# A two-layer decoder on one core: attention outputs turned, stored and split 18 to 22 chunks later, turned queries read two chunks later, one mask product on GpSimd

## The chip, the core and the metric

The kernel runs on one core of a Trainium2 chip. TensorE (PE) multiplies, with weight loads (PEld) beside the matmuls; VectorE (DVE), ScalarE (ACT) and GpSimd (POOL) do the elementwise work; SyncE (SP) issues the transfers. The metric is the device time of one execution in microseconds (us); less is better.

## The reference

A batch of one sequence of 256 tokens passes through two layers, all in f32. What matters here is the mixer of a layer:

```
proj = rms_norm(x) @ w_in          # 2048 -> 5632: q, k, v and four HGRN2 parts
q, k = rope(q), rope(k)            # 16 query heads, 4 key heads of 64
attn = rms_norm(sliding_window_attention(q, k, v, sinks), attn_gain)
f = lb + (1 - lb) * sigmoid(hf);  k_in = (1 - lb) * sigmoid(-hf)
o = hgrn2_chunkwise(silu(hq), k_in, hi, log f)     # gated linear recurrence, 8 heads of 128
hgrn = rms_norm(o, hgrn_gain) * silu(hg)
m = concat([attn, hgrn]) @ w_out   # then norm, residual, gated feed-forward, input embeddings
```

Attention has a window of 128: with 256 tokens in two blocks, block 0 sees its own keys, and block 1 sees its own keys under a lower triangle and those of block 0 under an upper one.

## The kernel before

Tokens stand in two tiles of 128 rows (t = 0 and 1). Every weight matrix is cut into strips of 512 columns, and a strip into chunks of 256 rows (512 KB). `load_w` (L264) loads a chunk into one of 4 raw buffers `wr`, ACT casts it to a rounded half `wh` (L174), and DVE subtracts to get the rest, `wl` (L175); there are 8 buffers of each half. `strip` (L274) runs 12 matmuls of 512 columns per chunk: for two k-tiles and two token tiles, activation-high by weight-high (L286), activation-low by weight-high (L287) and activation-high by weight-low (L289). So PE can go on with a chunk only when its cast and its subtraction are done; below, the subtraction of chunk n is called sub n, and chunks are counted from the start of a layer's input projection. Chunks 0 to 7 are keys and values, 8 to 23 queries (two halves of 8 heads), 24 to 31 the gate f of the first group of recurrence heads, 32 to 39 its q, 40 to 47 its i, 48 to 55 its g, and 56 to 87 the same for the second group.

All the rest of a layer is woven into the strips. `tick` (L94) is called once per chunk; `later(n, fn)` traces `fn` n ticks later, and generators started with `start` do one piece per tick. The order in which each engine runs its instructions is then set by a list scheduler: what is traced earlier has the higher priority, and an instruction goes where its inputs and its buffers allow it in the scheduler's own reckoning. A step that is traced later is therefore not held until then; it only gives way to what is traced ahead of it. Each engine executes its list in order, and SP's queue too.

A turn of data (`shuffled`, L208) is a transpose of 32x32 blocks on DVE (L215 or L218), a store to DRAM (L225) and four fetches (L231) that bring the blocks to their places. `attend` (L538), one generator per half and token tile, turns the queries, copies them into `qT` (L542), computes scores (L570), exponentials (L593), turns these, multiplies them by the masks in `masked` (L605; for t = 1 a product with `m_low` and one with `m_up`, both on DVE at L612), multiplies by the values (L621) and scales into `ao` (L624). After the second half it takes the norm, scales `ao` into two buffers (L551), turns them, and `split_shuffled` (L246) splits them into the high and low operands `ck` of the output projection: 4 products on ACT (L254) and 4 on DVE (L255) for each of the two buffers and each t. These operands are first read at the output projection, after chunk 87.

The recurrence (`Rec`, L637) turns f by transposes on PE (L657) into `f` and `k` by two sigmoids on ACT (L659, L660) and products on DVE (L663, L665), turns q (L680) into `qd`, and goes through doubling levels: L769, L772 and L774; L732 and L741 for levels 2 and 8, after `up` and `prepare` (L701 to L721); L797 for 32 and 64; L804; then outputs (L823, L824). `ao` shares its two buffers with the recurrence's `q` and `qd`, and `qT` with its `f` and `k`. The buffers `nat` for all passing data are 12, the PSUM buffers `ms` for all small matmuls 4.

Of the kernel before, what the change touches and what calls it, by code (L numbers as in the profile page):

```python
# [12 lines left out]
ALU = mybir.AluOpType  # L13
AX = mybir.AxisListType

P = 128
# [30 lines left out]
def decoder(ctx: ExitStack, tc: tile.TileContext, x, p, positions, w_in, attn_sinks,  # L47
# [16 lines left out]
    V, S, G, T = nc.vector, nc.scalar, nc.gpsimd, nc.tensor  # L64

    def tiny(n):
        return sm.tile([P, n], F32, tag="tiny", name="tiny", bufs=16)
# [4 lines left out]
    def later(n, fn):  # L72

        queue.append((clock[0] + n, fn))
# [3 lines left out]
    @contextmanager  # L78
    def behind(*names):

        with ExitStack() as st:
            for n in names:
                st.enter_context(tc.issue_after(marks[n].ins))
            yield
# [18 lines left out]
    def nat(shape=(P, W), dt=F32):  # L103
        return np_.tile(list(shape), dt, tag="nat", name="nat")

    def bank(shape=(P, W)):
        return pms.tile(list(shape), F32, tag="ms", name="ms")
# [38 lines left out]
    def gain_cols(base, l, n):  # L146
        return gT[:, base + l * n: base + (l + 1) * n]
# [24 lines left out]
    def split(src, hi, lo):  # L172

        a = S.copy(hi, src)  # L174
        v = V.tensor_tensor(lo, src, hi.bitcast(F32), op=ALU.subtract)  # L175
        return a, v
# [27 lines left out]
    def turn_order(a):  # L204

        return a.rearrange("p (q k i) -> p k q i", q=4, k=4)

    def shuffled(src, n=4, slow=True, ready=False):  # L208

        if ready:
            b = src
            V.transpose(b, b)  # L215
        else:
            b = nat((P, n * P))
            V.transpose(b.rearrange("p (q k j) -> p k q j", q=4, k=n),  # L218
                        src.rearrange("p (k q j) -> p k q j", k=n, q=4))
        m = dp.tile([4, 32, 4, n * 32], F32, tag="turn", name="turn")  # L220
        got = []

        def store():
            with behind("pe") if slow else nullcontext():
                nc.sync.dma_start(m.rearrange("a i q f -> (a i) (q f)"), b)  # L225

        def fetch():
            d = nat((P, n * P))
            with behind("pe") if slow else nullcontext():
                for q in range(4):  # L230
                    nc.sync.dma_start(d[q * 32:(q + 1) * 32].rearrange("i (a f) -> i a f", a=4),  # L231
                                      m[:, :, q].rearrange("a i f -> i a f"))
            got.append(d.rearrange("p (a k j) -> p k a j", a=4, k=n))
        if slow:
            later(1, store)
            later(2, fetch)
        else:
            store()
            fetch()
        return got  # L240

    def quarters(a):

        return a.rearrange("p k (a j) -> p k a j", a=4)

    def split_shuffled(d, gcols, hl, t):  # L246
        d, = d
        h, lo = (quarters(a[:, :, t * P:(t + 1) * P]) for a in hl)
        if gcols is None:
            split(d, h, lo)  # L250
            return
        for b in range(4):
            g = gcols[:, b:b + 1]
            marks["x"] = S.activation(h[:, b], d[:, b], AF.Copy, scale=g)  # L254
            V.scalar_tensor_tensor(lo[:, b], d[:, b], g, h[:, b].bitcast(F32),  # L255
                                   op0=ALU.mult, op1=ALU.subtract)
# [93 lines left out]
    m_low = cp.tile([P, P], F32, name="m_low")  # L350
    m_up = cp.tile([P, P], F32, name="m_up")
# [129 lines left out]
    for l in range(DEPTH):  # L481
# [55 lines left out]

        def attend(half, t, o):  # L538
            d = shuffled(o, ready=True)
            for _ in range(6):  # L540
                yield
            S.copy(quarters(qT[half][:, :, t * P:(t + 1) * P]), d[0])  # L542
            yield
            yield from head_pair(half, t)
            if half == 1:
                yield
                r = sum_rstd(ssa[t], 1024, f"ra{t}")
                d = []
                for h in range(2):
                    b = nat()  # L550
                    V.tensor_scalar(turn_order(b), ao[t][:, h].rearrange("p (k q i) -> p k q i", k=4, q=4),  # L551
                                    r[:, 0:1], None, op0=ALU.mult)
                    d.append(shuffled(b, ready=True))
                for _ in range(5):
                    yield
                for h in range(2):
                    split_shuffled(d[h], gain_cols(96, l, 8)[:, 4 * h:4 * h + 4], attn[h], t)

        def head_pair(half, t):

            q = qT[half]
            blocks = [t] if t == 0 else [t, t - 1]
            sc = {}
            for u in blocks:
                for g in range(2):
                    sc[u, g] = bank((P, 4, P))
                for j in range(4):
                    for g in range(2):
                        rows = slice(g * 64, (g + 1) * 64)
                        T.matmul(sc[u, g][:, j], q[rows, j, t * P:(t + 1) * P],  # L570
                                 kT[rows, half, u * P:(u + 1) * P], start=True, stop=True)
            ex, dens = [], []
            for g in range(2):
                kv = 2 * half + g
                hs = slice(kv * 4, kv * 4 + 4)
                st = nat()
                s_ = turn_order(st)

                def four(a):
                    return a.rearrange("p j (q i) -> p j q i", q=4)  # L580
                if t == 0:
                    V.tensor_tensor(s_, four(sc[t, g]),
                                    four(m_neg.unsqueeze(1)).to_broadcast([P, 4, 4, 32]), op=ALU.add)
                else:
                    S.copy(s_, four(sc[t, g]))
                    V.copy_predicated(s_, four(m_prev.bitcast(I32).unsqueeze(1))
                                      .to_broadcast([P, 4, 4, 32]), four(sc[t - 1, g]))
                nm = tiny(4)
                V.tensor_reduce(nm, s_, axis=AX.XY, op=ALU.max, negate=True)
                V.tensor_tensor(nm, nm, nsink[:, l, hs], op=ALU.min)  # L590
                den = tiny(4)
                for j in range(4):
                    S.activation(s_[:, j], s_[:, j], AF.Exp, bias=nm[:, j:j + 1],  # L593
                                 accum_out=den[:, j:j + 1])
                es = tiny(4)
                V.tensor_tensor(es, sink[:, l, hs], nm, op=ALU.add)
                S.activation(es, es, AF.Exp)
                V.tensor_tensor(den, den, es, op=ALU.add)
                V.reciprocal(den, den)
                ex.append(shuffled(st, ready=True))  # L600
                dens.append(den)
                if g == 0:
                    yield

            def masked(g):  # L605
                ec = nat((P, 4, P))
                if t == 0:
                    S.copy(quarters(ec), ex[g][0])
                    return [(t, ec)]
                ep = nat((P, 4, P))  # L610
                for e, m in ((ec, m_low), (ep, m_up)):
                    V.tensor_tensor(quarters(e), ex[g][0], quarters(m.unsqueeze(1))  # L612
                                    .to_broadcast([P, 4, 4, 32]), op=ALU.mult)
                return [(t - 1, ep), (t, ec)]

            def values(g, parts):
                kv = 2 * half + g
                po = bank((P, 4, 64))
                for j in range(4):
                    for i, (u, e) in enumerate(parts):  # L620
                        T.matmul(po[:, j], e[:, j], vv[:, u, kv * 64:(kv + 1) * 64],  # L621
                                 start=i == 0, stop=i == len(parts) - 1)
                dst = ao[t][:, half, g * 256:(g + 1) * 256]
                V.tensor_tensor(dst.rearrange("p (j d) -> p j d", d=64), po,  # L624
                                dens[g].unsqueeze(2).to_broadcast([P, 4, 64]), op=ALU.mult)
                square_sum(dst, ssa[t][:, kv:kv + 1], (P, 256))

            for _ in range(4):
                yield
            p0 = masked(0)  # L630
            yield
            values(0, p0)
            p1 = masked(1)
            yield
            values(1, p1)
# [375 lines left out]
```

## Time and profile before

| | |
|---|---|
| median of 3 runs | 2454.04 us (2452.37 to 2454.14) |
| the profiled execution | 2453.65 us, span 2451.9 us |
| PE busy | 2429.4 us (99%) |
| DVE, ACT, POOL busy | 1486.0, 1184.7, 101.2 us |
| DMA | 497.59 MB, mean 203 GB/s |
| granted TensorE clock, mean | 0.999 of full speed |

The two layers are at 0 to about 1250 us and from there to the end. The attention and the first group of the recurrence lie at 83 to 235 us in the first layer and at 1295 to 1445 us in the second. A matmul of 512 columns shows as 0.39 us of PE, but one starts every 0.23 us, since they are pipelined; busy time of PE therefore hides short waits, and its idle time is what is left of a wait after the pipeline has run dry.

### The profile page before, as it was taken

To read this page: it belongs to the slowest core of one execution; us is meant where nothing else is said; L and a number is where in the kernel's file an instruction comes from. 1 tells how busy PE (TensorE), PEld (TensorE's weight loads), DVE (VectorE), ACT (ScalarE), POOL (GpSimd) and SP (SyncE) were. 2 spreads that over 40 slices of the span, in tenths; PEclk is the share of its full clock that TensorE was granted. 3 is DMA by queue.
4 is the path that set the end of the run, shared out by engine and by line. 5 is a ranking of instruction groups with operands and counts; after the bars stand their busy time and mean duration, and the time that the engine had idled before them with its cause. 6 is when DMAs were issued, how large, how long until landed. Compare 5 with 4: busy or idle time off the path is not lost.

```text
span 2451.9 us, 30895 instructions
## 1 busy us (share of the span) xinstructions
PE 2429.4 (99%) x11245; PEld 2006.4 (82%) x11245; DVE 1486.0 (61%) x1991; ACT 1184.7 (48%) x1684; POOL 101.2 (4%) x213
## 2 busy tenths in 40 slices
PE   9999999999999999999999999999999999999999
PEld 7888887888888888887888888878888888888877
DVE  7678756554555555557666877565545555555674
ACT  6465445444444444446555554464444444344463
POOL 3100001000000000001010000010000000000010
PEclk9999999999999999999999999999999999999999
DMA  8657465766767766774776674657767677667754
GB/s 264 218 181 219 141 198 154 233 220 202 214 205 211 211 211 195 226 221 154 249 222 195 194 226 144 200 182 217 225 191 229 192 212 212 209 207 214 221 170 129
DMA packets 299064, 497.59 MB, mean 203 GB/s; under 512 B 23424, under 2 KB 68896, under 8 KB 298912
## 3 DMA queue, kind: packets, MB, share of 16 engines
q1 hardware_dynamic: 298608, 495.54, 66.0%
q8 instruction: 88, 1.44, 0.2%
q14 instruction: 64, 0.52, 0.1%
q10 hardware_dynamic: 240, 0.07, 0.0%
q0 software_dynamic: 64, 0.02, 0.0%
HBM read 470.38 MB, written 25.17 MB: 202 GB/s over the span
## 4 chain that ended last, share of the span: by engine, by line
PE 93%; DVE 3%; DMA 1%; ACT 1%; issue 1%; POOL 0%; SPq 0%; DVEq 0%; ACTq 0%; POOLq 0%
PE acc L286 30%; PE acc L287 30%; PE acc L289 29%; DMA wr<-in_w_in_dram 1%; PE ms L621 1%; PE ms L732 1%; DVE wl L175 1%; PE ms L189 0%; PE ms L570 0%; ACT junk L170 0%; PE ms L797 0%; ACT wh L174 0%; DVE ck L255 0%; PE ms L287 0%; PE ms L286 0%
## 5 line engine op out<-in xcount | busy, mean ns | idle before, releaser
L175 DVE TENSOR_TENSOR wl<-wr,wh 128x1024 fp32r<-128x1024 f32 x840 | 1024.4, 1223 | 839.2 <-ACT wh L174 831.1
L174 ACT CAST wh<-wr 128x1024 fp32r<-128x1024 f32 x840 | 882.1, 1053 | 1073.6 <-PE acc L287 919.7
L286 PE MATMUL acc<-wh,ck 128*128 128x512 f32 x3328 | 1302.2, 392 | 8.3 <-ACT ck L200 5.8
L289 PE MATMUL acc<-wl,ck 128*128 128x512 f32 x3328 | 1296.7, 390 | 5.0 <-DVE wl L175 5.0
L287 PE MATMUL acc<-wh,ck 128*128 128x512 f32 x3328 | 1300.3, 391 | 0.9 <-DVE ck L201 0.8
L286 PEld LDWEIGHTS acc<-wh,ck 128*128 128x128 f32 x3328 | 625.5, 188 | 143.9 <-ACT ck L200 10.8
L289 PEld LDWEIGHTS acc<-wl,ck 128*128 128x128 f32 x3328 | 625.8, 188 | 136.0 <-DVE wl L175 7.5
L287 PEld LDWEIGHTS acc<-wh,ck 128*128 128x128 f32 x3328 | 625.8, 188 | 134.4 <-DVE ck L201 4.4
L200 ACT ACTIVATE ck<-ms,gT 128x128 fp32r<-128x128 f32 x176 | 55.7, 369 | 25.4 <-DVE ck L201 15.2
L201 DVE SCALAR_TENSOR_TENSOR ck<-ms,gT,ck 128x128 fp32r<-128x128 f32 x176 | 53.8, 347 | 16.8 <-ACT ck L200 16.3
L160 POOL TENSOR_TENSOR tiny<-ssf 128x1 f32<-128x1 f32 x4 | 2.1, 536 | 1359.5 <-ACT junk L170 1359.2
L930 DVE TENSOR_TENSOR macc<-acc,macc 128x512 f32<-128x512 f32 x48 | 33.0, 688 | 5.1 <-PE acc L289 4.5
L897 ACT ACTIVATE nat<-acc,ry 128x512 f32<-128x512 f32 x44 | 30.2, 686 | 10.7 <-PE acc L289 10.7
L218 DVE STREAM_TRANSPOSE nat<-nat 128x512 f32<-128x512 f32 (+1 forms) x48 | 32.7, 681 | 2.6 <-POOL nat L515 2.6
L170 ACT ACTIVATE junk<-x 128x512 f32<-128x512 f32 x48 | 30.3, 630 | 7.3 <-DVE x L322 4.1
L903 DVE SCALAR_TENSOR_TENSOR nat<-acc,ry,nat 128x512 f32<-128x512 f32 x44 | 32.4, 748 | 0.1
L175 DVE TENSOR_TENSOR ck<-nat,ck 128x512 fp32r<-128x512 f32 x46 | 31.6, 687 | 1.2 <-ACT ck L174 1.1
L174 ACT CAST ck<-nat 128x512 fp32r<-128x512 f32 x46 | 28.4, 618 | 5.5 <-DVE nat L181 3.8
L215 DVE STREAM_TRANSPOSE nat<-nat 128x512 f32<-128x512 f32 x32 | 22.1, 703 | 14.4 <-POOL nat L515 8.0
L593 ACT ACTIVATE nat<-nat,tiny 128x128 f32<-128x128 f32 x64 | 24.9, 393 | 6.5 <-DVE tiny L590 6.5
L254 ACT ACTIVATE ck<-nat,gT 128x128 fp32r<-128x128 f32 x72 | 22.8, 392 | 9.7 <-DMA nat<-turn 9.6
L515 POOL TENSOR_TENSOR nat<-nat 128x256 f32<-128x256 f32 (+1 forms) x24 | 21.5, 917 | 111.3 <-DVE nat L508 63.2
(194 smaller groups left out, 894.4 us busy)
## 6 DMA issues: line engine op xcount, KB each, us to landing
wr<-in_w_in_dram SPq DMA_DIRECT2D x176, 512.0 KB, 4.6
wr<-in_w_ffn_gate_dram SPq DMA_DIRECT2D x176, 512.0 KB, 4.4
wr<-in_w_ffn_up_dram SPq DMA_DIRECT2D x176, 512.0 KB, 4.5
wr<-in_w_ffn_down_dram SPq DMA_DIRECT2D x176, 512.0 KB, 4.3
wr<-in_w_out_dram SPq DMA_DIRECT2D x64, 512.0 KB, 3.9
wr<-in_w_ple_gate_dram SPq DMA_DIRECT2D x64, 512.0 KB, 4.4
turn<-nat SPq DMA_DIRECT2D x86, 256.0 KB, 2.6
nat<-turn SPq DMA_DIRECT2D x344, 64.0 KB, 3.1
```

What stands on the lines that cost most here:

```text
L170: S.activation(j[:, 0:shape[1]], src, AF.Square, accum_out=acc)
L174: a = S.copy(hi, src)
L175: v = V.tensor_tensor(lo, src, hi.bitcast(F32), op=ALU.subtract)
L200: marks["x"] = S.activation(h[:, b], ps[:, b], AF.Copy, scale=g)
L201: V.scalar_tensor_tensor(lo[:, b], ps[:, b], g, h[:, b].bitcast(F32), op0=ALU.mult, op1=ALU.subtract)
L218: V.transpose(b.rearrange("p (q k j) -> p k q j", q=4, k=n), src.rearrange("p (k q j) -> p k q j", k=n, q=4))
L286: T.matmul(ps[t], xh, hi[:, k], start=first, stop=False)
L287: T.matmul(ps[t], xl, hi[:, k], start=False, stop=False)
L289: marks[t, c] = marks["pe"] = T.matmul(ps[t], xh, lo[:, k], start=False, stop=last)
L897: S.activation(gate[t], ps, AF.Silu, scale=rx2(t)[:, 0:1])
L903: V.scalar_tensor_tensor(gate[t], ps, rx2(t)[:, 0:1], gate[t], op0=ALU.mult, op1=ALU.mult)
L930: V.tensor_tensor(m, ps, m, op=ALU.add)
```

## The change

Four edits in `attend` and `masked`. The copy into `qT` is traced 8 ticks after the turn of the queries instead of 6, and with it all that follows it in the generator. The turn of the two scaled attention outputs (transpose, store and fetch) is traced 18 ticks (t = 0) or 22 ticks (t = 1) after the scaling, where it was traced at once. The splits follow 5 and 6 ticks after that, one buffer at a time; they were both traced 5 ticks after the turn. In `masked`, the product with `m_up` is traced first and runs on GpSimd; the one with `m_low` stays on DVE.

```
-            for _ in range(6):
+            for _ in range(8):
                 yield
             S.copy(quarters(qT[half][:, :, t * P:(t + 1) * P]), d[0])
...
-                    d.append(shuffled(b, ready=True))
-                for _ in range(5):
+                    d.append(b)
+                for _ in range(18 + 4 * t):
                     yield
+                d = [shuffled(b, ready=True) for b in d]
                 for h in range(2):
+                    for _ in range(5 - 4 * h):
+                        yield
                     split_shuffled(d[h], gain_cols(96, l, 8)[:, 4 * h:4 * h + 4], attn[h], t)
...
-                for e, m in ((ec, m_low), (ep, m_up)):
-                    V.tensor_tensor(quarters(e), ex[g][0], quarters(m.unsqueeze(1))
-                                    .to_broadcast([P, 4, 4, 32]), op=ALU.mult)
+                for e, m, en in ((ep, m_up, G), (ec, m_low, V)):
+                    en.tensor_tensor(quarters(e), ex[g][0], quarters(m.unsqueeze(1))
+                                     .to_broadcast([P, 4, 4, 32]), op=ALU.mult)
```

Lines below L553 have a number higher by 3 in the changed kernel (L680 of before is L683 there, L769 is L772, L174 and L175 keep theirs). No instruction is added but table loads on ACT (below); matmuls, transfers and products are the same in number.

The first place is DVE in the first layer, from the turned q (`qd`, L687 before, L690 after) to the first level (L772 before, L775 after). Before:

```order
L687 TENSOR_TENSOR qd<-qd,f 128x4x64
L689 TENSOR_TENSOR q<-qd,f 128x4x128
L672 SCALAR_TENSOR_TENSOR nat<-acc_1391,rx_561,nat 128x512
L175 TENSOR_TENSOR wl<-wr,wh 128x1024
L255 SCALAR_TENSOR_TENSOR ck<-nat,gT,ck 128x128 x2
L687 TENSOR_TENSOR qd<-qd,f 128x4x64
L689 TENSOR_TENSOR q<-qd,f 128x4x128
L255 SCALAR_TENSOR_TENSOR ck<-nat,gT,ck 128x128 x2
L772 TENSOR_TENSOR at<-ms,ident 128x256 x2
L255 SCALAR_TENSOR_TENSOR ck<-nat,gT,ck 128x128 x4
```

The same place in the changed kernel:

```order
L675 SCALAR_TENSOR_TENSOR nat<-acc_1310,rx_561,nat 128x512
L551 TENSOR_SCALAR nat<-ao_151,ra_1677 128x4x4x32 x2
L175 TENSOR_TENSOR wl<-wr,wh 128x1024
L690 TENSOR_TENSOR qd<-qd,f 128x4x64
L692 TENSOR_TENSOR q<-qd,f 128x4x128
L690 TENSOR_TENSOR qd<-qd,f 128x4x64
L692 TENSOR_TENSOR q<-qd,f 128x4x128
L775 TENSOR_TENSOR at<-ms,ident 128x256 x2
```

The L255 products of the split have left this stretch, and the scaling of `ao` for t = 1 (L551), which was done before it, now stands right ahead of `qd`.

The second place is ACT in the first layer, from the first sigmoid of f to the last one of the first group. Before:

```order
L659 ACT_TABLE_LOAD
L659 ACTIVATE f<-ms 128x4x128
L170 ACTIVATE junk,ssa_152<-ao_150 128x256
L660 ACTIVATE k<-ms 128x4x128
L170 ACTIVATE junk,ssa_152<-ao_150 128x256
L659 ACTIVATE f<-ms 128x4x128
L170 ACTIVATE junk,ssa_153<-ao_151 128x256
L660 ACTIVATE k<-ms 128x4x128
L174 CAST wh<-wr 128x1024 x4
```

In the changed kernel (L596 are the exponentials, L662 and L663 the sigmoids):

```order
L662 ACT_TABLE_LOAD
L662 ACTIVATE f<-ms 128x4x128
L596 ACT_TABLE_LOAD
L596 ACTIVATE nat,tiny<-nat,tiny 128x4x32 x4
L600 ACTIVATE tiny<-tiny 128x4
L596 ACTIVATE nat,tiny<-nat,tiny 128x4x32 x4
L600 ACTIVATE tiny<-tiny 128x4
L596 ACTIVATE nat,tiny<-nat,tiny 128x4x32 x4
L600 ACTIVATE tiny<-tiny 128x4
L663 ACT_TABLE_LOAD
L663 ACTIVATE k<-ms 128x4x128
L662 ACTIVATE f<-ms 128x4x128
```

Three of the four groups of exponentials of the second half of the heads now stand between the first two sigmoids, with two more table loads; the last cast ahead of the piece is chunk 43's, with the first group of exponentials between them, and the next four casts (44 to 47) come after one more sigmoid.

The third place is ACT where the second group of the recurrence turns its f (chunk 68 of the layer). Before:

```order
L254 ACTIVATE ck<-nat,gT 128x128 x4
L174 CAST wh<-wr 128x1024 x2
L659 ACTIVATE f<-ms 128x4x128
L660 ACTIVATE k<-ms 128x4x128
L174 CAST wh<-wr 128x1024
L659 ACTIVATE f<-ms 128x4x128
L660 ACTIVATE k<-ms 128x4x128
```

In the changed kernel:

```order
L254 ACTIVATE ck<-nat,gT 128x128 x15
L662 ACTIVATE f<-ms 128x4x128
L663 ACTIVATE k<-ms 128x4x128
L254 ACTIVATE ck<-nat,gT 128x128
L174 CAST wh<-wr 128x1024 x2
L662 ACTIVATE f<-ms 128x4x128
L663 ACTIVATE k<-ms 128x4x128
```

The splits that were moved run into those of the recurrence's own output here, and the casts of chunks 69 and 70 now stand behind the first two sigmoids, which read what PE transposes at chunk 68.

## Rows read from the trace of the kernel before

**Rows 1.** The page, part 1: busy us (share of the span) xinstructions of each engine.
```profile
PE 2429.4 (99%) x11245; PEld 2006.4 (82%) x11245; DVE 1486.0 (61%) x1991; ACT 1184.7 (48%) x1684; POOL 101.2 (4%) x213
```
**Rows 2.** Windows: stretch, its us, busy us (xinstructions) of PE, PEld, DVE, ACT, POOL; clock; DMA.
```profile
150.00:170.00 20.00, 18.63 (x111) 15.47 (x110) 15.85 (x36) 11.86 (x22) 2.62 (x8) 1.00 0.59 183
170.00:192.00 22.00, 19.60 (x96) 16.38 (x95) 22.00 (x55) 12.42 (x25) 0.00 (x0) 1.00 0.56 161
...
1382.00:1404.00 22.00, 19.99 (x97) 16.71 (x96) 22.00 (x55) 12.18 (x25) 0.00 (x0) 1.00 0.57 161
```
**Rows 3.** Timeline of PE, start us, us, what, [idle before <-releaser]; two of six waits.
```profile
163.82 0.50 PE L289 MATMUL acc<-wl,ck 128*128 128x512 f32 x1 [0.60 <-DVE wl L175]
...
190.62 0.50 PE L289 MATMUL acc<-wl,ck 128*128 128x512 f32 x1 [1.71 <-DVE wl L175]
```
**Rows 4.** Lines of DVE, 83 to 200 us: operation, xcount | busy us, mean ns | idle before.
```profile
L175 DVE TENSOR_TENSOR wl<-wr,wh 128x1024 fp32r<-128x1024 f32 x26 | 31.5, 1217 | 8.8 <-ACT wh L174 8.8
L215 DVE STREAM_TRANSPOSE nat<-nat 128x512 f32<-128x512 f32 x14 | 9.7, 702 | 5.0 <-ACT nat L593 3.4 <-POOL nat L515 1.6
...
L255 DVE SCALAR_TENSOR_TENSOR ck<-nat,gT,ck 128x128 fp32r<-128x128 f32 x16 | 4.7, 346 | 0.0
...
L612 DVE TENSOR_TENSOR nat<-nat,m_up 128x512 f32<-128x512 f32 x4 | 2.7, 682 | 0.0
```
**Rows 5.** Timeline of PE: two subtraction-fed matmuls a chunk apart, and chunk 43's first.
```profile
140.06 0.39 PE L289 MATMUL acc<-wl,ck 128*128 128x512 f32 x1
...
142.78 0.39 PE L289 MATMUL acc<-wl,ck 128*128 128x512 f32 x1
...
147.76 0.39 PE L286 MATMUL acc<-wh,ck 128*128 128x512 f32 x1
```
**Rows 6.** Chain that ended last, start us, us, what: small matmuls on PE, DVE's L741.
```profile
122.86 1.73 PE ms L621 x16
...
185.85 2.25 DVE at L741 x10
...
260.34 0.87 PE ms L680 x8
263.95 2.60 PE ms L769 x16
272.00 2.67 PE ms L732 x16
```
**Rows 7.** Timeline of ACT, first layer.
```profile
88.39 1.28 ACT L593 ACT_TABLE_LOAD   x1
89.68 0.40 ACT L593 ACTIVATE nat<-nat,tiny 128x128 f32<-128x128 f32 x1
...
91.33 0.60 ACT L542 COPY qT<-nat 128x512 f32<-128x512 f32 x1
...
110.56 0.62 ACT L542 COPY qT<-nat 128x512 f32<-128x512 f32 x1 [5.90 <-DMA nat<-turn]
...
137.31 1.06 ACT L174 CAST wh<-wr 128x1024 fp32r<-128x1024 f32 x1
...
231.98 1.05 ACT L174 CAST wh<-wr 128x1024 fp32r<-128x1024 f32 x1 [1.66 <-PE acc L287]
```
**Rows 8.** Timeline of DVE: the ends of the stretches summed below.
```profile
162.25 0.39 DVE L624 TENSOR_TENSOR ao<-ms,tiny 128x256 f32<-128x256 f32 x1
...
182.92 0.42 DVE L721 TENSOR_TENSOR qf<-qf,f 128x256 f32<-128x256 f32 x1
...
196.60 1.22 DVE L175 TENSOR_TENSOR wl<-wr,wh 128x1024 fp32r<-128x1024 f32 x1
```
**Rows 9.** Timeline of POOL, and of DVE, around the rotation of the queries (L515).
```profile
71.35 1.72 POOL L515 TENSOR_TENSOR nat<-nat 128x256 f32<-128x256 f32 x1
...
95.81 1.43 POOL L515 TENSOR_TENSOR nat<-nat 128x256 f32<-128x256 f32 x2 [18.40 <-DVE nat L508]
...
70.81 1.66 DVE L175 TENSOR_TENSOR wl<-wr,wh 128x1024 fp32r<-128x1024 f32 x1 [0.30 <-ACT wh L174]
```

## The prediction

> **What bounds the kernel now.** I read the page's busy line first. PE is busy 99% of the span, DVE 61%, ACT 48% and GpSimd 4% [rows 1]. So no shorter work on DVE, ACT or GpSimd is worth anything by itself: only time in which PE stands idle can be won back, and the change gives PE neither more nor less to do. Then the windows of the stretch that the change touches. In 150 to 170 us PE is busy 18.63 of 20 us, in 170 to 192 19.60 of 22, and in the same place of the second layer, 1382 to 1404, 19.99 of 22 [rows 2]: idle 1.37 + 2.40 + 2.01 = 5.78 us. In two of the three windows DVE is busy 22.00 of 22 us while the clock is at its full level (1.00) and DMA at 0.56 or 0.57. The timeline of PE says what the idle time is: L289 waits for `wl`, the subtraction on DVE, 0.60 us at 163.82 and 1.71 us at 190.62 [rows 3]. So for these 40 us, where attention, its splits and the first recurrence group meet, DVE is the bound, and the rest of DVE's idle 39% cannot help it. These 5.78 us are all that the change can win directly. Against 2454 us that is 0.24%; the measurement can tell about 0.2%, 4.9 us, from no change.
>
> **What leaves DVE.** Per layer the change takes three things out of this stretch of DVE. (1) Sixteen products of the split, L255: 0.35 us each as busy time [rows 4], but ten products of L741 take 2.25 us together [rows 6], 0.23 each, since they overlap. Between 0.23 and 0.35 I take 0.27: 4.3 us. (2) Three of the four turns of the scaled outputs, L215 of 0.70 us [rows 4]: 2.1 us. One is still done early in the new order. (3) Two of the four `m_up` products of 0.68 us [rows 4] lie in the second half of the heads, the nearer one: 1.4 us. Together some 7.8 us per layer, against an idle time of 3.77 us in layer 1 and 2.01 in layer 2. By this alone everything would be won.
>
> **What comes nearer.** The list order takes it back in part. With those products gone, the recurrence's steps move ahead: counted in the two orders, the first `qd` matmul L680 goes from the middle of chunk 47 to the end of chunk 44, L769 from chunk 49 to 46.5, and the two L732 from 51.5 and 54.5 to 49 and 52. PE then reaches a matmul that needs DVE's result 2.25 to 2.75 chunks sooner, with that much less work in front of it. So I compare, leg by leg, what DVE must do between two points at which PE waits for it with what PE has to do there. A chunk is 2.72 us of PE (140.06 to 142.78) [rows 5], a piece of L680 0.87, L769 2.60, L732 2.67 [rows 6].
>
> Leg 1, from the last attention output to the first L732. On DVE it was 162.25 to 183.34, 21.1 us [rows 8]. Out of it go nine L255 (2.4), one L215 (0.7) and, as it covers fewer chunks, two subtractions of 1.22 [rows 4] (2.4); one residual product leaves and one small product comes, about level. That is 15.6 us, or up to 16.6 if DVE must wait once for L769. PE has 4.5 chunks, two L680 and one L769 there: 12.2 + 1.7 + 2.6 = 16.5. Leg 2, from the first L732 to the second: DVE took 185.85 [rows 6] to 196.60 [rows 8], 10.8 us; two more of the L741 products make it 11.2. PE has one L732 and three chunks, 2.67 + 8.16 = 10.8: 0.4 late. The shorter legs behind it come out within 0.3 us of nought by the same reckoning. So I leave 0.4 us per layer; the margins are thin, and each us that DVE loses in a leg is a us of time per layer.
>
> **GpSimd's product.** No row shows a product of 128x512 on GpSimd. The nearest is L515, 128x256: two of them 1.43 us, and one beside a subtraction 1.72 us, where that subtraction took 1.66 [rows 9] against a mean of 1.22 [rows 4]. So DVE saves 0.68 per product at best, and at worst loses as much as GpSimd takes, 1.43 by two halves. I take the subtraction's own loss, 0.44 of the 0.68, so 0.24 saved; both fall ahead of leg 1, where subtractions are a chunk or more early, so the sum does not move by it. The Trainium skill, "SBUF — State Buffer", section "Who interferes with whom", speaks against this edit: DVE operations with two inputs from SBUF and GpSimd lock each other out of a shared port. The trace agrees, in the 1.72 and 1.66 us named above. By the rule alone the edit would win nothing on DVE, and by the lead nothing would be lost either.
>
> **ACT.** Three groups of four exponentials now stand between the first two sigmoids of f, with two more table loads, and no cast between. A group is 89.68 to 91.33, 1.65 us; a load 1.28; a sigmoid is priced like the 128x512 copy, 0.60 [rows 7]. From the cast of chunk 43 to that of chunk 44 inclusive: 4 x 1.65 + 3 x 1.28 + 4 x 0.6 + 1.06 = 13.9 us. Cover: that cast ends at 138.37 [rows 7], and PE takes up its chunk at 147.76 [rows 5], a lead of 9.4; to this come a chunk, 2.72, and two L621 of 1.73 [rows 6], in all 15.6. So 1.7 us remain. The later `qT` should widen it: ACT stood 5.90 us at 110.56 for the turned queries [rows 7], and what of this goes is lead for all the casts behind, up to 7.6 us in all. I cost it at nothing; without the cover it costs what w, the wait of these exponentials for scores, goes beyond 1.7 us.
>
> **The score banks.** One subtraction now stands between the last L624 of the first half and the scaling that PE's next scores hang on: 0 to 1.22 us per layer, taken as 0.25, since that subtraction is due anyway.
>
> **The moved turns and splits.** Four transposes, stores and sixteen fetches per layer move on SP's queue past some 20 chunks of weights, with the 32 products of the split (16 on ACT, 16 on DVE). They land where the ring of eight cast buffers is full: at 231.98 the cast waits 1.66 us for PE to free one [rows 7]. There DVE and ACT have 15 us in hand and the work costs nothing; the operands are not read until chunk 88. One spot is dear: at chunk 68 the casts of chunks 69 and 70 now queue behind two sigmoids that wait for PE's transposes of that very chunk. Two sigmoids 1.2, a piece of the split 0.3, the cast 1.06 and the subtraction 1.22 make 3.8 us; PE has 2.72 and the small matmuls behind, 0.87 by the nearest row, in all 3.6 [rows 5, 6]. I take 0.3 per layer, from 0 (cast let through in time) to 1.2 (one subtraction late).
>
> **Sum.** Against the profiled execution of 2453.65 us (span 2451.9, 1.75 around it): minus 5.78, plus 2 x (0.4 + 0.25 + 0.3) = 1.9, gives minus 3.9. The median is 0.39 above that execution, so 2454.04 - 3.9 = 2450.1, rounded to 2450.0.
>
> **Rivals.**
> A, the forecast: 2447.8 to 2452.5 with the bounds above (0 to 2.2 us left idle per layer, a little more than nothing regained). Chance 0.42.
> B, the leads hold everywhere: all idle goes, and so does what PE loses in restarting its pipeline after each wait. The idle counts only what is left when the pipeline has run dry; with six waits at one start gap of 0.2 us each some 1.2 us come on top: 2454.04 - 5.8 - 1.2 = 2447.0, 2446 to 2448. For it: 7.8 us leave DVE where 2 to 4 are missing. Against: PE's demands come 2.5 chunks nearer. Chance 0.17.
> C, the waits only move: DVE is one subtraction and one GpSimd collision later in legs 1 and 2 than I reckon, 1.2 + 0.4 to 0.8, or the splits' late spot costs its 1.2 too. That gives 1.6 to 3.2 per layer on top of the forecast: 2453 to 2457, no change. For it: margins of 0.9 and -0.4 us. Chance 0.20.
> D, the other side: the run of exponentials without a cast starves PE. The groups of exponentials stand in a fixed order behind the first sigmoid, each waiting for PE's scores and for DVE's scaling; if those come a chunk apart (2.72 us) three groups wait w = 5 to 8 us. The price is 2 x (w - 1.7) on top of 2450: slower by more than 4.9 us from w = 6.2 on, 2462.6 at w = 8. For it: the order holds the casts 44 to 47 behind all of it. Against: the lead may be 6 us larger by the shorter wait at `qT`. Chance 0.17, counted from w = 6.2 on.
> E, dearer table loads: 2454 to 2456. In the trace the next exponential starts at 89.68, 0.01 us behind the end of the load, so nothing is drained there [rows 7]; were each load 1.4 us dearer, the 1.7 us of cover would turn into a loss of 2.4 per layer, 2454.8. The Trainium skill, "ScalarE: Activation LUTs", section "What ACT_TABLE_LOAD costs", adds about 1.38 us of drain to each load; this trace does not show it. Chance 0.04.
> That the change does not do what it says applies in small: one of four turns stays early, and is counted so.
>
> **Numbers.** Faster by over 0.2% (below 2449.1): B, and 0.4 of A, 0.17 + 0.17 = 0.34. Slower by over 0.2% (above 2458.9): D, 0.17. Within: 0.49. The range 2446.5 to 2457.0 takes in A, C, E and most of B, and leaves out D and a few hundredths of B. The forecast's own range is 2447.8 to 2452.5.
>
> **What the changed profile would show.** Right: PE idle under 1 us in each layer's stretch from the last attention outputs to the second L732, with DVE no longer at 22 of 22 us; no wait of L286 for `wh` behind the exponentials; the copy into `qT` waiting far under 5.90 us; GpSimd products of about 1.4 us. C shows as waits of L289 for `wl` about as long as now, at L732 or at chunk 69 (some 240 us). D shows as waits of L286 for `wh` at chunks 44 to 47, about 150 us, and ACT waiting for `ms` in the exponentials. The forecast is wrong if PE's idle time in the stretch falls and the total does not: then something outside it has been moved too.

## The result: slower, and the profile after

The changed kernel takes 2457.70 us (median of 21 runs, 2455.05 to 2462.55), the kernel before 2452.94 us beside it: a ratio of 1.0018, 95% interval 1.0012 to 1.0024. That is 4.4 us slower by the ratio (4.8 by the medians), and its interval leaves out 1; the time lies above the predicted range (2446.5 to 2457.0), and the forecast was 4 us faster. The profiled execution took 2458.52 us, its span is 2456.6 us.

The page's busy line of the changed kernel, engine by engine as in [rows 1]:

```profile
PE 2432.4 (99%) x11245; PEld 2010.0 (82%) x11245; DVE 1483.3 (60%) x1983; ACT 1189.9 (48%) x1688; POOL 118.0 (5%) x221
```

It tells nothing: no share has moved by more than a point. The windows do. First the three of [rows 2], of the changed kernel (stretch, its us, busy us of PE, PEld, DVE, ACT and POOL, clock, DMA):

```profile
150.00:170.00 20.00, 19.35 (x114) 16.59 (x113) 15.63 (x31) 12.24 (x22) 8.50 (x10) 1.00 0.51 163
170.00:192.00 22.00, 22.00 (x108) 19.05 (x107) 22.00 (x46) 9.41 (x11) 0.00 (x0) 1.00 0.49 146
1382.00:1404.00 22.00, 22.00 (x109) 19.07 (x108) 21.98 (x45) 8.85 (x10) 0.00 (x0) 1.00 0.49 144
```

The idle time that the change was to win is gone: 0.65 us is left where 5.78 was, and that 0.65 is another wait (it comes again in the second layer, 0.67 us, ahead of the window). DVE is still busy 22 of 22 us, but no longer late. So the time has been lost elsewhere, and the timeline of PE shows where, at the first scores of the layer (start, us, what, idle before and its releaser):

```profile
90.03 2.05 PE L573 MATMUL ms<-kT,qT 64*128 64x128 f32 x24
93.93 2.04 PE L573 MATMUL ms<-kT,qT 64*128 64x128 f32 x8 [1.85 <-DVE nat L585]
...
1309.36 0.83 PE L573 MATMUL ms<-kT,qT 64*128 64x128 f32 x10 [1.58 <-DVE nat L585]
```

PE has started the scores of t = 1 and stands until DVE has added the mask (L585) to a score of t = 0, which frees the score bank: 1.85 us in the first layer, 1.58 in the second. In the first layer the granted clock then falls to the lower of its two levels. The windows around the wait, columns as above:

```profile
92.00:94.00 2.00, 0.15 (x2) 0.10 (x1) 1.47 (x3) 1.66 (x8) 0.47 (x1) 0.92 1.05 406
94.00:96.00 2.00, 2.00 (x9) 1.78 (x9) 2.00 (x8) 0.00 (x0) 0.00 (x0) 0.50 1.09 346
...
98.00:100.00 2.00, 2.00 (x6) 1.52 (x6) 1.58 (x3) 1.90 (x10) 0.00 (x0) 0.50 0.01 3
100.00:102.00 2.00, 2.00 (x9) 1.64 (x8) 1.04 (x5) 0.68 (x1) 0.00 (x0) 0.87 0.47 141
```

From 0.92, 0.50 three times (the row left out is one) and 0.87 over 2 us each, PE was at half clock for 0.3 + 6 + 0.5 = 6.8 us, which is 3.4 us of work: more than the wait itself. In the second layer the clock stayed at 1.00 around its 1.58 us.

Why DVE is late stands in its own timeline of the changed kernel, with GpSimd's rotation between:

```profile
87.56 0.65 DVE L585 TENSOR_TENSOR nat<-ms,m_neg 128x512 f32<-128x512 f32 x1
...
88.14 0.68 DVE L508 TENSOR_TENSOR nat<-acc,rot 128x512 f32<-128x512 f32 x1
...
90.14 2.32 POOL L515 TENSOR_TENSOR nat<-nat 128x256 f32<-128x256 f32 x2 [3.25 <-DVE tiny L593]
...
92.50 0.71 DVE L215 STREAM_TRANSPOSE nat<-nat 128x512 f32<-128x512 f32 x1 [0.69 <-POOL nat L515]
...
93.14 0.65 DVE L585 TENSOR_TENSOR nat<-ms,m_neg 128x512 f32<-128x512 f32 x1
```

Two mask additions free the two banks of t = 0. Between them now stand the rotation (L508) and the turn (L215) of the second half's queries, and the turn waits for GpSimd. Before, both additions stood together, ahead of all that, and the scores of t = 1 ran without a break:

```profile
84.36 1.29 DVE L582 TENSOR_TENSOR nat<-ms,m_neg 128x512 f32<-128x512 f32 x2 [1.49 <-PE ms L570]
...
91.99 2.06 PE L570 MATMUL ms<-kT,qT 64*128 64x128 f32 x32
```

The other waits that are new are of PE for GpSimd's mask product and for the recurrence's `qf`:

```profile
135.43 1.75 PE L573 MATMUL ms<-kT,qT 64*128 64x128 f32 x16 [0.27 <-DVE nat L585]
...
163.99 1.22 PE L624 MATMUL ms<-vv,nat 128*128 128x64 f32 x9 [0.65 <-POOL nat L615]
...
275.54 2.74 PE L735 MATMUL ms<-qf,k 128*128 128x192 f32 x15 [0.79 <-DVE qf L724]
...
1491.84 2.40 PE L735 MATMUL ms<-qf,k 128*128 128x192 f32 x13 [1.42 <-DVE qf L724]
```

What each place is worth can be read by comparing when the same weight matmul, by its number in the kernel, starts in the two traces. At the first scores the changed kernel falls back by 6.0 us in the first layer and 2.1 in the second. From there to the end of the first recurrence group it wins 3.7 and 0.7. At L735 it loses 1.0 and 1.6.

### The profile page after: what moved, and what is told of

The parts are those of the page before. It is cut to its first block, busy times and chain, and to the rows that moved or that the text cites. A ratio compares the mean times of both kernels' runs of the same rounds, so it can differ in the third digit from the quotient of the medians.

```text
span 2456.6 us, 30958 instructions
## 1 busy us (share of the span) xinstructions
PE 2432.4 (99%) x11245; PEld 2010.0 (82%) x11245; DVE 1483.3 (60%) x1983; ACT 1189.9 (48%) x1688; POOL 118.0 (5%) x221
## 4 chain that ended last, share of the span: by engine, by line
PE 93%; DVE 2%; DMA 2%; ACT 1%; issue 1%; POOL 1%; SPq 0%; DVEq 0%; ACTq 0%; POOLq 0%
PE acc L286 29%; PE acc L287 29%; PE acc L289 29%; DMA wr<-in_w_in_dram 2%; PE ms L735 1%; PE ms L624 1%; DVE wl L175 1%; ACT wh L174 1%; PE ms L189 0%; PE ms L800 0%; ACT junk L170 0%; PE ms L286 0%; PE ms L289 0%; PE ms L287 0%; DVE x L322 0%
## 5 line engine op out<-in xcount | busy, mean ns | idle before, releaser
L175 DVE TENSOR_TENSOR wl<-wr,wh 128x1024 fp32r<-128x1024 f32 x840 | 1024.9, 1224 | 809.4 <-ACT wh L174 803.7
L174 ACT CAST wh<-wr 128x1024 fp32r<-128x1024 f32 x840 | 882.3, 1054 | 1069.4 <-PE acc L287 903.9
L289 PE MATMUL acc<-wl,ck 128*128 128x512 f32 x3328 | 1298.6, 391 | 0.0
L289 PEld LDWEIGHTS acc<-wl,ck 128*128 128x128 f32 x3328 | 626.0, 188 | 129.2 <-DVE wl L175 0.3
L175 DVE TENSOR_TENSOR ck<-nat,ck 128x512 fp32r<-128x512 f32 x46 | 31.5, 687 | 0.1
L255 DVE SCALAR_TENSOR_TENSOR ck<-nat,gT,ck 128x128 fp32r<-128x128 f32 x72 | 21.4, 350 | 16.2 <-ACT ck L254 13.5
L174 ACT CAST ck<-nat 128x512 fp32r<-128x512 f32 x46 | 28.4, 619 | 3.7 <-DVE nat L181 3.5
L627 DVE TENSOR_TENSOR ao<-ms,tiny 128x256 f32<-128x256 f32 x16 | 6.8, 424 | 37.9 <-PE ms L624 37.8
L215 DVE STREAM_TRANSPOSE nat<-nat 128x512 f32<-128x512 f32 x32 | 22.6, 708 | 10.4 <-POOL nat L515 7.0
```

The costliest lines, as they stand in the source:

```text
L289: marks[t, c] = marks["pe"] = T.matmul(ps[t], xh, lo[:, k], start=False, stop=last)
```

## The experiments

Each kernel was timed in five rounds beside the kernel before, whose median was 2452.4 to 2452.7 us. The theory to be tested: the later `qT` alone makes the loss. A layer's queries come in two halves of 8 chunks. With 6 ticks and one more, the first half's scores are traced 7 ticks after its queries, ahead of the second half's rotation at 8; with 8 and one more they are traced at 9, behind it, and lose their priority.

**One edit at a time.** Only the later `qT`, against the kernel before:

```
-            for _ in range(6):
+            for _ in range(8):
                 yield
             S.copy(quarters(qT[half][:, :, t * P:(t + 1) * P]), d[0])
```

> Only the copy into qT is traced 8 ticks after the turn instead of 6; splits and masks as before. Theory 1 (the later qT costs: the turn of the other half's queries goes on DVE ahead of the mask addition that frees a score bank): PE waits 1.5 to 2 us for L582 at the first scores, about 94 us and 1309 us, in both layers, and the attention's own waits at L289 shrink from 5.8 us to between 1 and 4; ratio to before 1.001 to 1.0025 (+2.5 to +6 us). Theory 2 (the later turns and splits cost, by the lead of the casts lost at chunk 68): no such wait here, ratio 0.998 to 1.000. Theory 3 (the masks on GpSimd cost): as theory 2.

Measured: 2467.87 us, ratio 1.0065 (1.0052 to 1.0077), 15 us slower, far more than any theory had. The wait at the first scores is there (1.84 and 1.57 us). But the waits at L289 did not shrink, they grew, from 5.0 us in both layers to 8.0; the first layer's are here, with those behind them:

```profile
184.60 0.50 PE L289 MATMUL acc<-wl,ck 128*128 128x512 f32 x1 [0.95 <-DVE wl L175]
188.13 2.84 PE L732 MATMUL ms<-qf,k 128*128 128x192 f32 x16 [0.52 <-DVE qf L721]
194.27 0.50 PE L289 MATMUL acc<-wl,ck 128*128 128x512 f32 x1 [3.29 <-DVE wl L175]
196.27 0.93 PE L797 MATMUL ms<-q,k 128*32 128x32 f32 x14 [0.81 <-DVE k L759]
```

In this kernel's trace the first L680 stands at chunk 45.7 (before 47.3) and the second L732 at 51.3 (before 54.5), with the splits' products still on DVE. So the later `qT` alone brings the recurrence nearer; in the whole change, where the splits have gone too, these waits do not come.

The change without the later `qT`, against the changed kernel:

```
-            for _ in range(8):
+            for _ in range(6):
                 yield
             S.copy(quarters(qT[half][:, :, t * P:(t + 1) * P]), d[0])
```

> The change without the later qT (6 ticks as before), with the later turns and splits and m_up on GpSimd. Theory 1: no wait at the first scores, the 5.8 us at L289 mostly gone, the waits of L735 (0.8 us at about 275, 1.4 us at 1492 in the changed kernel) stay; ratio 0.998 to 0.9995 (-1 to -5 us). Theory 2: the loss stays, ratio 1.001 to 1.002. Theory 3: the same as theory 2, with waits of PE for DVE near the masks.

Measured: 2445.58 us, ratio 0.9972 (0.9961 to 0.9984), 7 us faster than before: the later `qT` costs 12 us by the medians. The windows of [rows 2] in this kernel:

```profile
150.00:170.00 20.00, 20.00 (x125) 17.82 (x124) 16.77 (x36) 13.51 (x24) 5.63 (x9) 1.00 0.45 133
170.00:192.00 22.00, 22.00 (x109) 19.16 (x108) 21.87 (x47) 8.57 (x9) 0.00 (x0) 1.00 0.52 158
1382.00:1404.00 22.00, 22.00 (x137) 17.96 (x136) 21.14 (x41) 10.90 (x14) 0.00 (x0) 1.00 0.56 173
```

PE idles 0.00 of 64 us. Its first scores run in one piece, and its L680 stands at chunk 47.6, no earlier than before (47.3) although the splits have gone.

Only the later turns and splits, against the kernel before (the edit is the second hunk of the change's diff):

```
-                    d.append(shuffled(b, ready=True))
-                for _ in range(5):
+                    d.append(b)
+                for _ in range(18 + 4 * t):
```

> Only the later turns and splits; qT at 6 ticks, both masks on DVE. Theory 1: waits of L735 of 0.5 to 1.5 us per layer near 275 and 1492 us, less wait at L289 (from 5.8 us to under 3 us); ratio 0.998 to 1.000 (-5 to 0 us). Theory 2: ratio 1.001 to 1.002. Theory 3: ratio 0.998 or below, better than with the masks.

Measured: 2450.08 us, ratio 0.9990 (0.9981 to 0.9999): a gain of 2.5 us. Only the product with `m_up` on GpSimd, against the kernel before:

```
-                for e, m in ((ec, m_low), (ep, m_up)):
-                    V.tensor_tensor(quarters(e), ex[g][0], quarters(m.unsqueeze(1))
+                for e, m, en in ((ep, m_up, G), (ec, m_low, V)):
+                    en.tensor_tensor(quarters(e), ex[g][0], quarters(m.unsqueeze(1))
```

> Only the product with m_up moved to GpSimd. Theory 1: within 0.9995 to 1.0005 (1 us either way), GpSimd products of 1.3 to 3.6 us each. Theory 2: the same. Theory 3: ratio 1.001 or more, by waits of PE for DVE in the stretch 120 to 165 us.

Measured: 2453.52 us, ratio 1.0002 (0.9993 to 1.0011): nothing. So theories 2 and 3 fall as causes of the loss: neither the splits nor the mask alone makes the kernel slower. But what theory 2 named does happen in the kernel with the splits alone. The cast of chunk 70 waits 3.42 us there for its weights, that of chunk 71 stands behind four sigmoids and eight splits, and PE waits for it and then for a subtraction:

```profile
247.65 0.50 PE L286 MATMUL acc<-wh,ck 128*128 128x512 f32 x1 [0.62 <-ACT wh L174]
...
249.93 0.80 PE L289 MATMUL acc<-wl,ck 128*128 128x512 f32 x1 [1.07 <-DVE wl L175]
```

By the starts of its matmuls this kernel wins 4.7 us up to chunk 66 of the first layer and loses 3.8 of them again by chunk 76 (1.7 of it by a lower clock behind these waits). And the two edits do not add up: 2.5 us and nothing alone, 7 together.

**Which half of the heads.** The changed kernel with 8 ticks for the first half only, then for the second only:

```
-            for _ in range(8):
+            for _ in range(8 - 2 * half):
```

> The changed kernel with qT traced 8 ticks after the turn for the first half of the heads and 6 for the second. Theory 1a (the loss of 12 us against the change without the later qT sits at the first scores, which only the first half's delay moves behind the turn of the second half's queries): PE waits 1.5 to 2 us near 94 and 1309 us; 2449 to 2456 us, ratio 0.9985 to 1.0015. Theory 1b (it sits in the recurrence, which the second half's delay brings nearer): near the change without the later qT, 2445 to 2448 us, ratio 0.997 to 0.998.

```
-            for _ in range(8):
+            for _ in range(6 + 2 * half):
```

> The changed kernel with qT traced 6 ticks after the turn for the first half and 8 for the second. Theory 1a: no wait at the first scores, 2445 to 2449 us, ratio 0.997 to 0.9985. Theory 1b: waits of PE at L624, L735 and L289 between 150 and 280 us and the same in the second layer, 2450 to 2456 us, ratio 0.999 to 1.0015.

Measured: 2454.58 us (1.0006, 0.9997 to 1.0015) and 2453.99 us (1.0002, 0.9993 to 1.0011). Against 2445.58 with neither, each half costs 8 to 9 us, and both together 12: each theory had part of it, and the parts do not add up. The first half's delay brings the wait at the scores (1.84 and 1.57 us). The second half's brings something else, PE waiting for a cast:

```profile
141.97 0.50 PE L286 MATMUL acc<-wh,ck 128*128 128x512 f32 x1 [0.97 <-ACT wh L174]
143.92 0.67 PE L289 MATMUL acc<-wl,ck 128*128 128x512 f32 x1 [0.75 <-DVE wl L175]
```

ACT's timeline in the same kernel shows the run of exponentials and table loads before it:

```profile
128.80 1.05 ACT L174 CAST wh<-wr 128x1024 fp32r<-128x1024 f32 x1
...
131.51 1.28 ACT L662 ACT_TABLE_LOAD   x1
...
138.12 1.28 ACT L663 ACT_TABLE_LOAD   x1
...
140.86 3.89 ACT L174 CAST wh<-wr 128x1024 fp32r<-128x1024 f32 x4
```

No cast starts for 12 us, with 8.3 us in hand (that at 128.80 ends at 129.85, and PE takes up its chunk at 138.12). That is what rival D described, in the first layer, at chunk 40 instead of 44. In this profile these two waits, 1.7 us at a lower clock behind them, two waits for GpSimd's product (0.66 and 0.73) and two at L735 (1.03 and 0.90) make 6.7 of the 8.4 us.

**How far, and what for.** The change without the later `qT` and with 12 and 16 ticks, then with 8 and 12:

```
-                for _ in range(18 + 4 * t):
+                for _ in range(12 + 4 * t):
```

> The change without the later qT, with the turns of the attention outputs traced 12 and 16 ticks after the scaling instead of 18 and 22. If the lead of the casts that is lost at chunk 68 is what is left (0.57 us of L735 at 1479 us, 0.19 us at 250 us): these waits go or stay under 0.3 us, 2444 to 2446 us, ratio 0.9965 to 0.9975. If the early half of the splits, now at chunks 55 and 56 on DVE, delays the recurrence again: waits of L289 or L800 between 190 and 215 us, 2447 to 2450 us, ratio 0.998 to 0.999.

```
-                for _ in range(18 + 4 * t):
+                for _ in range(8 + 4 * t):
```

> The change without the later qT, with the turns of the attention outputs traced 8 and 12 ticks after the scaling. In the order the splits stand at chunks 51 to 57 and 68, and 75 casts stand ahead of the first sigmoid of the second group, as before the change. If the splits need only leave the stretch up to the second L735: 2444 to 2447 us, ratio 0.9965 to 0.998. If splits at chunk 51 and 52 delay the levels of the recurrence: waits of L289 at 170 to 200 us again, 2447 to 2451 us, ratio 0.998 to 0.9995.

Measured: 2446.56 us (0.9970, 0.9959 to 0.9982), level with 18 (the waits of 0.57 and 0.19 us are gone, one of 0.44 at 202.90 is new), and 2452.36 us (1.0000, 0.9991 to 1.0008), nothing left of the gain. With 8 ticks the splits fall among the levels of the recurrence, and PE waits at the second of the two L735:

```profile
187.68 2.60 PE L735 MATMUL ms<-qf,k 128*128 128x192 f32 x9 [3.21 <-DVE qf L724]
```

The mask: the changed kernel with both products on DVE, in the old order, and the change without the later `qT` with both on DVE, `m_up` first:

```
-                for e, m, en in ((ep, m_up, G), (ec, m_low, V)):
-                    en.tensor_tensor(quarters(e), ex[g][0], quarters(m.unsqueeze(1))
+                for e, m in ((ec, m_low), (ep, m_up)):
+                    V.tensor_tensor(quarters(e), ex[g][0], quarters(m.unsqueeze(1))
```

> The changed kernel with both mask products on DVE. If the product on GpSimd relieves DVE (the splits alone came to 2450 us and with the GpSimd product to 2446): 2459 to 2463 us, ratio 1.0025 to 1.0045. If GpSimd's product, 1.3 to 3.6 us each beside DVE's, costs more than it saves: 2453 to 2456 us, ratio 1.000 to 1.0015.

```
-                for e, m, en in ((ep, m_up, G), (ec, m_low, V)):
+                for e, m, en in ((ep, m_up, V), (ec, m_low, V)):
```

> The change without the later qT, with the m_up product traced first but on DVE. If GpSimd's taking the product is what made 2446 us out of the 2450 us of the splits alone: 2448 to 2452 us, ratio 0.998 to 0.9998. If only the order of tracing did: 2444 to 2447 us, ratio 0.9965 to 0.998.

Measured: 2455.68 us (1.0009, 1.0000 to 1.0018), 2 us less than with GpSimd, but the two intervals overlap, so no difference is shown; and 2452.23 us (1.0000, 0.9991 to 1.0009), 6.6 us more than with GpSimd, which is clear. What the product on GpSimd is worth hangs on the order around it. In the second kernel PE waits for the subtraction again (1.26 us at 159.95), which it does not with the product on GpSimd; in the changed kernel PE waits for GpSimd instead. Nor is the second run a test of GpSimd alone: the swap moved the first L683 (the L680 of before) from chunk 47.6 to 45.75, so the order changed with the engine.

**The place of the second mask addition.** The changed kernel, with the additions of both score banks traced at once; nothing else is edited:

```
...
+            st0 = []
+            if t == 0:
+                for g in range(2):
+                    st0.append(nat())
+                    V.tensor_tensor(turn_order(st0[g]), four(sc[t, g]),
+                                    four(m_neg.unsqueeze(1)).to_broadcast([P, 4, 4, 32]), op=ALU.add)
             for g in range(2):
...
-                st = nat()
+                st = st0[g] if t == 0 else nat()
...
-                    V.tensor_tensor(s_, four(sc[t, g]),
-                                    four(m_neg.unsqueeze(1)).to_broadcast([P, 4, 4, 32]), op=ALU.add)
+                    pass
```

> The changed kernel, with the two mask additions of a t = 0 piece (m_neg, one for each score bank) traced together at once, where the second was traced a tick after the first; on DVE the second then stands ahead of the second half's rotation and turn. If that place holds the score bank and so makes the wait at the first scores: no wait of PE over 0.3 us near 94 and 1309 us, 2449 to 2454 us, ratio 0.9985 to 1.0008. If the wait comes of the scores themselves standing 0.75 chunk earlier on PE: 1 us of wait or more stays, 2455 to 2458 us, ratio 1.001 to 1.002.

Measured: 2450.06 us, ratio 0.9990 (0.9981 to 0.9999). That is 7.6 us less than the changed kernel. DVE's two additions and PE's scores in this kernel:

```profile
87.99 1.25 DVE L583 TENSOR_TENSOR nat<-ms,m_neg 128x512 f32<-128x512 f32 x2
...
90.47 2.06 PE L573 MATMUL ms<-kT,qT 64*128 64x128 f32 x32
```

The scores stand as early on PE as in the changed kernel (at chunk 25.8, against 26.7 with 6 ticks), and there is no wait: the place of one addition of 0.65 us made it. The same edit with `qT` at 6 ticks, where both additions stood together already:

> The same with qT at 6 ticks. There the two additions already stood together, so by the first theory nothing changes against the change without the later qT: 2444 to 2447 us, ratio 0.9965 to 0.998. By the second the same.

Measured: 2445.63 us, ratio 0.9975 (0.9964 to 0.9985), the same as without it. The version to keep is the change without the later `qT`; the 12-tick one is level with it.

## Why the prediction was wrong, step by step

**The step that failed** is the price of the later `qT`: "The later `qT` should widen it", costed "at nothing", from ACT's queue alone. What it said of ACT was right. From the cast of chunk 43 to the end of chunk 44's it had 13.9 us; the rows are these:

```profile
137.56 1.06 ACT L174 CAST wh<-wr 128x1024 fp32r<-128x1024 f32 x1
...
140.28 1.28 ACT L662 ACT_TABLE_LOAD   x1
141.57 0.60 ACT L662 ACTIVATE f<-ms 128x512 f32<-128x512 f32 x1
...
151.28 3.90 ACT L174 CAST wh<-wr 128x1024 fp32r<-128x1024 f32 x4
```

The first cast ends at 138.62, and the first of the four, a quarter of 3.90 us, at about 152.3: 13.6 us, and PE waited for no cast here. The copies of the second half into `qT` wait for nothing now, where ACT stood 5.90 us before. Traced later, they even run earlier, since the second half's rotation and turn have moved ahead on DVE:

```profile
105.02 0.62 ACT L542 COPY qT<-nat 128x512 f32<-128x512 f32 x1
...
110.50 0.61 ACT L542 COPY qT<-nat 128x512 f32<-128x512 f32 x1
```

Before, these two stood at 110.56 [rows 7] and 122.43. The sigmoid starts 0.01 us behind the load's end, so rival E's dearer load did not come. The Trainium skill ("ScalarE: Activation LUTs", section "What ACT_TABLE_LOAD costs") gives a drain of about 1.38 us with each load; it is not seen here either.

But the delay was followed only to the queue where its own wait stood. "And with it all that follows it in the generator": the scores and mask additions of the first half went along, past the second half's rotation, and this place, chunks 24 to 27, was not looked at. The sum has a term for a score bank that comes free late, 0.25 us per layer, but only for the second half's scores; at the first half's the same kind of wait was 1.85 and 1.58 us, and 3.4 us more at the lower clock.

Of the 12 us that the later `qT` costs, 7.6 went with the place of the second mask addition: in the profiled execution the waits and the lower clock just named make 6.8, and the waits at L735 (0.79 and 1.42 us) are gone too. The other 4.4 us (2450.06 against 2445.63) come with the delay as a whole once that addition is mended; in that kernel PE waits 0.73 us per layer at the last product with the values, for GpSimd's mask product, and 0.4 at the second half's scores, 2.3 us in all. The profiled executions of these two kernels are 3.8 us apart in span, and by the starts of the same matmuls 2.2 of that lie between chunks 20 and 88 of the two layers. Of the rest, 1.3 lie at a wait near 405 us, where PE waits for ACT to write the operands of a later product: every kernel here has it, at 1.2 to 2.7 us, and whether the delay lengthens it is open.

**The splits: right with the mask edit, and more.** 5.78 us of idle time went, as worked out, and the change without `qT` came out at 2445.58, below rival B's 2447.0. So B, not the forecast, held for these edits. By the starts of the same matmuls that kernel wins 7.2 us between chunks 20 and 88 of the two layers (5.3 and 1.9), more than the idle time that went, as B had it. But the splits alone came to 2450.08: near the forecast's number, by other steps, since they won the stretch and lost at chunks 70 to 76. The sum, in which GpSimd's product moves nothing, missed the 4.5 us between these two kernels. With the product on GpSimd, PE loses only 0.5 us at chunks 70 to 76, and what in the order makes that difference is open.

**What comes nearer: the effect right, the cause wrong.** The prediction put the earlier L680 and L732 down to the products that had gone. Two runs show the later `qT` as the cause: alone it moves L680 to chunk 45.7; without it L680 stays at 47.6. (It is not the only edit that can: the swap of the mask product's engine moved it to 45.75 too.) The legs themselves came out: at the two L732 of the first group PE waits for nothing. A whole order was compared where three edits should each have been built by itself.

**GpSimd's product: bounds too narrow, and on one side only.** It was looked for on DVE. PE waits for it directly, 0.65 us at 163.99 and 0.67 in the second layer. Its rows, with the subtractions and the other product beside it:

```profile
153.06 4.62 DVE L175 TENSOR_TENSOR wl<-wr,wh 128x1024 fp32r<-128x1024 f32 x4
...
157.94 1.43 DVE L615 TENSOR_TENSOR nat<-nat,m_low 128x512 f32<-128x512 f32 x1
...
155.24 3.58 POOL L615 TENSOR_TENSOR nat<-nat,m_up 128x512 f32<-128x512 f32 x1 [20.41 <-DMA nat<-turn]
...
162.66 1.28 POOL L615 TENSOR_TENSOR nat<-nat,m_up 128x512 f32<-128x512 f32 x1
```

It takes 1.28 us, near the 1.43 of [rows 9], but 3.58 beside subtractions, and `m_low` 1.43 where the two overlap, 0.68 in the other piece. The four subtractions took 4.62 us, no more than their mean of 1.22 [rows 4], so against these GpSimd did the yielding. The Trainium skill ("SBUF — State Buffer", section "Who interferes with whom") has GpSimd and two-input operations of DVE lock each other out; the trace agrees, in the 3.58 us against 1.28.

**Score banks.** 0.25 us per layer was taken; 0.27 at 135.43 and a second short wait make 0.44 and 0.38. Right in size, for the second half.

**Chunk 68.** Costed at 0.3 us per layer for the one cast that waits. What it missed is the lead. ACT's timeline of the changed kernel:

```profile
226.73 1.03 ACT L174 CAST wh<-wr 128x1024 fp32r<-128x1024 f32 x1
...
246.10 0.60 ACT L662 ACTIVATE f<-ms 128x512 f32<-128x512 f32 x1 [6.25 <-PE ms L660]
...
247.36 1.99 ACT L174 CAST wh<-wr 128x1024 fp32r<-128x1024 f32 x2
```

For 20 us no cast runs, because the next ones stand behind a sigmoid that waits for chunk 68. The cast of chunk 68 is done 18.1 us before PE takes up its chunk, that of chunk 69 only 0.6. PE waits for neither, but the first L735 waits 0.79 and 1.42 us for DVE: 2.2 us of the whole, against 0.6 in the sum. That the spent lead makes these waits, since the subtractions to be made up meet the second group's levels on DVE, is argued and not shown. With the two mask additions together no cast starts for 19 us either, the lead falls to 2.6 us at chunk 70, and L735 waits for nothing. What is shown is the plainer case above: with the splits alone the lead of chunk 71 falls to 0.05 us, and PE waits for the cast itself. The change without the later `qT` has a like order there, and loses 0.19 us at chunk 72 of the first layer and 0.57 at the second layer's L735.

**Rival D** got its mechanism right and its place wrong: it did not happen in the changed kernel, where the cast of chunk 43 ends at 138.62 and PE takes it up at 155.43, a lead of 16.8 us instead of 9.4, but it did, at chunk 40, when only the second half was delayed. In the changed kernel that lead was luck in part: the cast is no earlier than before (138.37), PE is late. With the two mask additions together PE comes at 149.82, and the lead is still 16.6 us, because the cast is done at 133.23.

## What to carry to other kernels

Where the order of tracing sets priorities, a delay counted in ticks is to be held against everything else that falls due within it: from 7 to 9 ticks is nothing, but the work at 8 has changed sides. Follow such a delay through all that hangs on it, to the next place where a buffer is freed, and build each edit alone before giving a cause to a shift in the order of them all. A shift of work into a full ring costs nothing only if the queue of the casts does not stop there: with the splits alone, two gaps of 11 us between casts were enough for PE to use up the whole lead.

## What the chip showed unexpectedly

A wait of PE can cost more than itself, and not each time. Waits of 1.84 and 1.85 us at the same place were followed by a clock of 0.50 for 6.8 us in the changed kernel and by 1.00 throughout in the kernel with the later `qT` alone; in the latter the clock fell to 0.50 behind the wait of 3.29 us at 194.27. With `qT` delayed for the first half alone, the wait of 1.84 us was followed by windows of 0.75, 0.50 and 0.89, which is 1.7 us of work; with both mask products on DVE the same 1.84 us were followed by 1.00. So the price of such a wait lay between its own length and 3.4 us more, and a single profile does not give it.
